# The first S5 block and the first GLA head in written order on VectorE and ScalarE, with their tables loaded early

## The chip, the cores and the metric

One Trainium2 chip, one core. The metric is the time of one execution of the program in device microseconds (us). The median of 3 runs of the kernel before is 879.52 us (878.79 to 879.74). The engines are called PE (TensorE), DVE (VectorE), ACT (ScalarE), POOL (GpSimd) and SP (SyncE); here POOL and SP mostly issue DMAs.

## What is computed

A decoder block on 512 tokens with 16 meta tokens ahead of them, width 1024. One projection `w_in` gives q, k, v, r, a low-rank gate, u and two gates z. Two mixers run beside each other: gated linear attention (GLA, 4 heads) and a grouped complex-diagonal state space model (S5, 64 groups of 16 channels with 64 states). Their outputs are gated and merged, and a squared-ReLU MLP follows.

```
proj = rmsnorm(h) @ w_in
q, k, v, r, a_low, u, z_gla, z_ssm = split(proj)
# GLA, per head and chunk of 64:
b = cumsum(log_a);  q_in = q*exp(b - b_ref);  k_in = k*exp(b_ref - b)
o = tril(q_in @ k_in.T) @ v + (q*exp(b)) @ state
state = exp(b_last)*state + (k*exp(b_last - b)).T @ v
# S5, per group:
x_t = Lbar x_{t-1} + Bbar u_t;   y_t = Re(C x_t) + D u_t
# merge and MLP:
mixed = sigmoid(z_gla)*(norm(o)*silu(r) @ w_o) + sigmoid(z_ssm)*glu(gelu(y))
h = h + rmsnorm(mixed @ w_out);   h = h + rmsnorm(relu(rmsnorm(h) @ w_ff1)**2 @ w_ff2)
```

## The kernel before

All dense products are in fp32 by three passes: each weight tile of 128 columns is loaded raw by SP (`wraw`, three buffers, `raw_w`, L166), split into a high part on ACT (`whi`, L160) and a low part on DVE (`wlo`, L175), and PE multiplies hi by hi, hi by lo and lo by hi of the normalised input `xh`, `xl` (`feat_tile`, `mm3`, L61). One such product, its split and what follows it is a slot: `slot()` takes the next of the list `dense`; `early_slot()` also works off a list of small jobs, each with an estimate of its cost on DVE.

The program has an early phase and a main phase. In the early phase the u, z and low-rank columns are multiplied, while jobs compute the S5 parameters: powers of lambda (written to DRAM as `lamd` by `powers_out`), the input matrix B (`b_bar`, to `bard`), and the decay sums of the heads (`bd`). The order of PE is pinned throughout to the order in which the code is written. The orders of DVE and ACT are pinned in the early phase only: there `V` and `S` are wrappers that keep each instruction in written order. The early phase ends with the two slots that carry `blocks[0].tables()`; then `V, S = nc.vector, nc.scalar`, and a scheduler orders the rows of DVE and ACT from there on. On the chip each engine works through its rows in the order in which they stand.

The main phase is a loop over the 8 S5 blocks of 8 groups each. Beside the first four blocks one GLA head each is computed. Per block:

- `loads` (L1095, L1097): B (512 KB) and lambda's powers `lam` (2 x 256 KB) are read from DRAM, spread over the partitions. Block 0 loads on POOL's queue, all others on SP's.
- `tables` (L1105 to L1119): M2 (a copy and five DVE rows) and M1 (four DVE rows, from B and lam). The tables of a block are computed during the block before.
- `turns` (L1124 to L1130, L235 to L238): `d0` and `E` are filled by ACT, eight loads bring `U`, and twelve DVE rows double `E` three times.
- `kernels` (L1142 to L1145): the local kernel `krow`, to DRAM, and back as M3 on POOL.
- `scan` (L1167 to L1177): `v` from M1 and U, copies `vs` of exchanged halves on ACT, the scan row on DVE (L1172), then X in three rows.

Per head (`Head`): `decays` (L964 to L985) loads `b2` and takes three differences, all in one buffer `d1`, and their exponentials on ACT: `e_gk`, `e_k`, `e_q`, `e_fk`, `e_fq`, `e_dec`; `query_decay` adds `e_gq`. The slots value, value, key, query give `vt`, `kT` and the queries; `key` multiplies kT into `e_gk`, `e_k`, `e_fk` (L997 to L999), `query` the queries into `e_q`, `e_fq`, `e_gq` (L1005 to L1007). `turn_values` and `turn_keys` transpose on PE (L66), `scores` reads `e_k`, `e_q`, `e_fk`, `e_fq`, and `states` the turned keys and values (L1038 to L1053).

On PE, block 0 and head 0 run in this order: value slot, kernels, value slot, scan, key slot, turn_values, query slot, turn_keys, a gate slot, scores and states; then the first value slot of block 1.

SP issues its DMAs in one row too: weight tiles in the order of the slots, and between them U, b2, and B and lam.

Of the kernel before, what the change touches and what calls it, by code (L numbers as in the profile page):

```python
# [10 lines left out]
F32R = mybir.dt.float32r  # L11
# [6 lines left out]
P = 128  # L18
# [19 lines left out]
T8 = 8  # L38
# [12 lines left out]
def hybrid_block(ctx: ExitStack, tc: tile.TileContext, io, out: bass.AP):  # L51
# [814 lines left out]
    def b_bar(c):  # L866
# [8 lines left out]
        if c:  # L875
            for i, half_ in enumerate((low_, high_)):
                nc.gpsimd.dma_start(bard[T8 * i : T8 * i + T8].rearrange("h g n -> g h n"), bar[half_].rearrange("g h c n -> g h (c n)"))

    low_rank()
    gate_weights()  # L880
    ready.update({0: f0, 1: f1})
# [29 lines left out]
    early_slot(2.2, 2.2)  # L911
    early_slot(2.2, 100.0)
    assert not jobs
    sga.close()
    st5.close()

    sgb = ExitStack()
    pgb = pool("pgb", stack=sgb)
# [7 lines left out]
    G.memset(scb[0], 0.0)  # L926
    d0 = mk(b5, [P, GB, NST], tag="d0")
    G.memset(d0, 0.0)
    NS = 80
    metas = [mk(pgb, [NS, DV + P], F32R, tag=f"meta{i}") for i in range(2)]  # L930
    for t in metas:
        S.copy(t, d0[:NS].rearrange("p g c -> p (g c)")[:, : DV + P])

    class Head:

# [17 lines left out]
        def turn_values(self):  # L953
            self.vtok = mk(pgb, [P, TT, DV], tag="vtok", bufs=2)
            for j, vt in enumerate(self.vt):
# [3 lines left out]
                    PE.transpose(ps[:, t * P : (t + 1) * P], vt[:, t * P : (t + 1) * P], ident)  # L959
                S.copy(self.vtok[:, :, cc], ps.rearrange("p (t c) -> p t c", t=TT))  # L960

        def decays(self):
            b2 = mk(pgb, [P, NT], tag="b2")
            nc.sync.dma_start(b2, bd[self.h])  # L964
            bm = b2[:, :SEQ].rearrange("p (c t) -> p c t", t=CH)
            bp = b2[:, :SEQ].rearrange("p (c t) -> p c t", t=P)

            def ex(shape, src, tag, scale):
                e = mk(pgb, shape, tag="e_" + tag)
                S.activation(e, src, AF.Exp, scale=scale)  # L970
# [7 lines left out]
            V.tensor_sub(d1.rearrange("p (c t) -> p c t", t=CH), bm, bm[:, :, 32:33].to_broadcast([P, 8, CH]))  # L978
# [3 lines left out]
            V.tensor_sub(dx, bp, bp[:, :, 63:64].to_broadcast([P, TT, P]))  # L982
# [3 lines left out]
            self.b2, self.ex = b2, ex  # L986

        def query_decay(self):
            self.qg = self.ex([P, SEQ], self.b2[:, :SEQ], "gq", -1.0 / TAU)
# [51 lines left out]
        def states(self):  # L1041
            self.st = []
            for t in range(0, TT, 2):
                pst = bank().rearrange("p (t v) -> p t v", t=2)
                for i in range(t, t + 2):
                    k, v = (self.ktok[:, i - 1, :], self.vtok[:, i - 1, :]) if i else (self.kmeta, self.vmeta)
                    PE.matmul(pst[:, i % 2], k, v, start=True, stop=True)
                for i in range(t, t + 2):
                    st = mk(pgb, [P, DV], tag="st", bufs=4)
                    if i == 0:  # L1050
                        V.tensor_copy(st, pst[:, 0])
                    else:
                        V.scalar_tensor_tensor(st, self.st[-1], self.dec[:, i - 1 : i], pst[:, i % 2], op0=ALU.mult, op1=ALU.add)  # L1053
                    self.st.append(st)

        def outputs(self):
# [27 lines left out]
    class Block:  # L1084
# [6 lines left out]
        def loads(self, queue=nc.sync):  # L1091

            self.B = mk(b5, [P, GB, 2, NST_N], tag="B")
            self.lam = mk(b5, [P, 2, GB, NST_N], tag="lam")
            queue.dma_start(self.B.rearrange("p g c n -> p (g c n)"), bard[:, self.gs, :].rearrange("h g n -> h (g n)").unsqueeze(0).to_broadcast([T8, HG, GB * 2 * NST_N]))  # L1095
            for i in range(2):
                queue.dma_start(self.lam[:, i].rearrange("p g n -> p (g n)"), lamd[i, :, self.gs, :].rearrange("l g n -> l (g n)").unsqueeze(1).to_broadcast([T8, HG, GB * NST_N]))  # L1097

        def tables(self):

# [46 lines left out]
        def scan(self):  # L1147

            M3 = self.M3 = mk(b5, [P, GB, P], tag="M3", bufs=1)
            for sp in range(T8):  # L1150
                s = T8 - 1 - sp
                nc.gpsimd.dma_start(M3[sp * HG : (sp + 1) * HG], kpad[self.gs].rearrange("g h l -> h g l")[:, :, 112 - 16 * s : 240 - 16 * s])
            U, E = self.U, self.E
            v, vs = (mk(b5, [P, GB, NST], tag=t, bufs=1) for t in ("v", "vs"))

            def exchanged(src, gg):

                S.copy(vs[:64, gg], src[64:])
                S.copy(vs[64:, gg], src[:64])
# [12 lines left out]
            V.tensor_tensor_scan(flat, d0.rearrange("p g c -> p (g c)"), flat, 0.0, op0=ALU.mult, op1=ALU.add)  # L1172
            X = self.X = mk(b5, [P, GB, NST], tag="X", bufs=1)
            exchanged(v, slice(0, GB))
            V.tensor_mul(X, v, E[:, 0])
            V.tensor_mul(vs, vs, E[:, 1])
            V.tensor_sub(X, X, vs)  # L1177
# [78 lines left out]
    for kind in ("r0", "r1", "r2", "r3", "r4", "r5", "r6", "r7", "z7", *(f"o{m}" for m in range(KT))):  # L1256
# [10 lines left out]
    assert not jobs and next(first, None) is None  # L1267
    V, S = nc.vector, nc.scalar
    for b, blk in enumerate(blocks):
        this = heads[b] if b < HEADS else None  # L1270
        last = heads[b - 1] if 0 < b <= HEADS else None
        blk.turns()
        following = iter(())
        if b + 1 < NBLK:
            following = blocks[b + 1].tables()
        slot()
        blk.kernels()
        if b:
            blocks[b - 1].output()
# [4 lines left out]
        blk.scan()  # L1284
# [7 lines left out]
        if b:  # L1292
            next(following, None)
        if b < NBLK - 1:
            slot()
        if this:
            this.turn_values()
        if b:
            next(following, None)
        slot()  # L1300
        if this:
            this.turn_keys()
        if not b:
            with tc.issue_after(blk.made.ins):
                next(following, None)
                next(following, None)
# [12 lines left out]
        if this:  # L1319
            this.scores()  # L1320
            this.states()
        if b:
            blocks[b - 1].turn_output()
        next(following, None)
    slot()
    blocks[-1].output()
# [364 lines left out]
```

## Time and profile before

| | |
|---|---|
| median of the runs | 879.52 us (878.79 to 879.74) |
| the profiled execution | 879.33 us |
| its span | 877.4 us |
| granted clock of TensorE, mean | 0.996 |
| PE busy in the span | 864.0 us |
| DVE, ACT, POOL busy | 654.1, 442.6, 122.0 us |
| end of the early phase and block 0, head 0 | about 88 to 140 us of the span |

In the profile a row names the engine, the line, the operation and the tiles (out<-in, without their numbers, so that M is M1 or M2, and d is d0 or d1), then the shapes and the count. In timelines the first column is the start in us from the span's start, the second the duration, and square brackets show how long the engine was idle just before and what released it. The matmuls of a slot are one after another and overlap; the step from start to start is what one costs. DMA issues are rows of SP's and POOL's queues (SPq, POOLq).

### The profile page before, as it was taken

Reading aid. Unit: us, or ns where it says so; the run is one execution under the profiler, and the core shown is the slowest. Engines: PE = TensorE matmul, PEld = TensorE weight load, DVE = VectorE, ACT = ScalarE, POOL = GpSimd, SP = SyncE. Lnnn points to the kernel's source line nnn. Section 1 sums busy time; section 2 is a strip of 40 time slices with the busy share of each in tenths; the row PEclk is TensorE's granted clock in tenths of the full one; section 3 lists DMA queues with packets and bytes.
Section 4 is the critical chain, followed back from the end, with each engine's and each line's share of the span. In section 5 each row is a group of like instructions: output and inputs, shape, how many; then the busy total and the mean of one; then the engine's idle time right before and its main releaser. Section 6 shows DMA issues by size and latency. Waiting matters only on the chain.

```text
span 877.4 us, 13275 instructions
## 1 busy us (share of the span) xinstructions
PE 864.0 (98%) x4824; PEld 739.6 (84%) x4824; DVE 654.1 (75%) x1180; ACT 442.6 (50%) x749; POOL 122.0 (14%) x214
## 2 busy tenths in 40 slices
PE   9999989999999999999999999999999999999996
PEld 8998879998988888888888888988888888888885
DVE  6999988969696789966445765576766677788886
ACT  7677365757664555334334544333222236665763
POOL 1122120131304221342000001021112100000001
PEclk9999999999999999999999999999999999999999
DMA  9776885554555757758545761598999966866564
GB/s 316 236 223 181 214 202 150 133 143 139 138 138 146 231 151 199 209 153 290 156 145 175 234 164 69 171 322 289 338 296 313 322 228 238 266 196 199 172 204 141
DMA packets 166905, 180.57 MB, mean 206 GB/s; under 512 B 18056, under 2 KB 126760, under 8 KB 166840
## 3 DMA queue, kind: packets, MB, share of 16 engines
q1 hardware_dynamic: 147240, 117.00, 45.3%
q0 software_dynamic: 17744, 58.52, 19.8%
q10 hardware_dynamic: 1856, 4.20, 1.4%
q8 instruction: 38, 0.62, 0.3%
q14 instruction: 27, 0.22, 0.1%
HBM read 143.74 MB, written 35.95 MB: 205 GB/s over the span
## 4 chain that ended last, share of the span: by engine, by line
PE 93%; DMA 3%; DVE 2%; issue 1%; ACT 0%; SPq 0%; ACTq 0%; POOL 0%; DVEq 0%
PE mm L61 68%; PE sm L61 23%; PE sm L66 2%; DMA wraw<-in_w_in_dram 2%; DMA lam<-lamd 1%; DVE xT L79 0%; DVE wlo L79 0%; DVE c L1612 0%; DVE c L1606 0%; SPq L1097 0%; DVE M L79 0%; DVE v L1172 0%; DVE B L79 0%; DVE wlo L175 0%; DVE B L1117 0%
## 5 line engine op out<-in xcount | busy, mean ns | idle before, releaser
L160 ACT ACTIVATE whi<-wraw 128x1024 fp32r<-128x1024 f32 x87 | 92.2, 1060 | 224.8 <-PE mm L61 202.6
L175 DVE TENSOR_TENSOR wlo<-wraw,whi 128x1024 fp32r<-128x1024 f32 x87 | 106.4, 1223 | 107.8 <-ACT whi L160 105.8
L61 PE MATMUL mm<-xh,whi 128*128 128x512 f32 (+2 forms) x464 | 159.4, 344 | 0.0
L61 PE MATMUL mm<-xh,wlo 128*128 128x512 f32 (+2 forms) x464 | 156.2, 337 | 0.0
L61 PE MATMUL mm<-xl,whi 128*128 128x512 f32 (+2 forms) x464 | 156.1, 336 | 0.0
L61 PE MATMUL mm<-hh,whi 128*128 128x512 f32 (+1 forms) x280 | 104.0, 371 | 0.0
L61 PE MATMUL mm<-hl,whi 128*128 128x512 f32 (+1 forms) x280 | 103.8, 371 | 0.0
L61 PE MATMUL mm<-hh,wlo 128*128 128x512 f32 (+1 forms) x280 | 103.8, 371 | 0.0
L61 PEld LDWEIGHTS mm<-xh,whi 128*128 128x128 f32 x464 | 88.0, 190 | 9.7 <-issue 1.2
L61 PEld LDWEIGHTS mm<-xh,wlo 128*128 128x128 f32 x464 | 87.8, 189 | 9.2
L61 PEld LDWEIGHTS mm<-xl,whi 128*128 128x128 f32 x464 | 87.9, 189 | 8.5
L1549 DVE TENSOR_TENSOR wlo<-wraw,whi 128x1024 fp32r<-128x1024 f32 x56 | 68.4, 1223 | 20.3 <-ACT whi L1545 20.3
L61 PE MATMUL sm<-wlo,fh 128*128 128x512 f32 x192 | 74.8, 390 | 0.0
L61 PE MATMUL sm<-whi,fh 128*128 128x512 f32 x192 | 74.7, 389 | 0.0
L61 PE MATMUL sm<-whi,fl 128*128 128x512 f32 x192 | 74.7, 389 | 0.0
L1545 ACT ACTIVATE whi<-wraw 128x1024 fp32r<-128x1024 f32 x56 | 58.6, 1049 | 16.8 <-PE mm L61 11.7
L61 PEld LDWEIGHTS mm<-hh,wlo 128*128 128x128 f32 x280 | 52.7, 188 | 9.1
L61 PEld LDWEIGHTS mm<-hl,whi 128*128 128x128 f32 x280 | 52.8, 188 | 9.0
L61 PEld LDWEIGHTS mm<-hh,whi 128*128 128x128 f32 x280 | 52.8, 188 | 9.0
L160 ACT ACTIVATE fh<-f 128x512 fp32r<-128x512 f32 x48 | 30.3, 631 | 45.0 <-PE sm L61 29.9
L61 PE MATMUL mm<-gh,whi 128*128 128x512 f32 x128 | 49.8, 389 | 0.0
L61 PE MATMUL mm<-gl,whi 128*128 128x512 f32 x128 | 49.8, 389 | 0.0
(408 smaller groups left out, 1777.3 us busy)
## 6 DMA issues: line engine op xcount, KB each, us to landing
wraw<-in_w_ff_dram SPq DMA_DIRECT2D x56, 512.0 KB, 4.6
wraw<-in_w_in_dram SPq DMA_DIRECT2D x46, 512.0 KB, 4.1
w2raw<-in_w_ff_dram POOLq DMA_DIRECT2D x16, 1024.0 KB, 8.8
t2d<-w2t POOLq DMA_DIRECT2D x16, 1024.0 KB, 5.9
wraw<-t2d SPq DMA_DIRECT2D x32, 512.0 KB, 4.0
wraw<-in_w_glu_dram SPq DMA_DIRECT2D x16, 512.0 KB, 4.3
M<-kpad POOLq DMA_DIRECT2D x64, 64.0 KB, 2.6
wraw<-in_w_o_gla_dram SPq DMA_DIRECT2D x8, 512.0 KB, 6.2
```

Source lines behind the costliest of these rows:

```text
L61: ins = nc.tensor.matmul(*args, **kw)
L66: ins = nc.tensor.transpose(*args, **kw)
L160: S.activation(dst, src, AF.Copy, scale=scale)
L175: V.tensor_sub(lo, raw, f32(hi))
L1545: halved = S.activation(bh, raw, AF.Copy)
L1549: V.tensor_sub(bl, raw, f32(bh))
```

## The change

- Written order goes on. The lines `V, S = nc.vector, nc.scalar` move behind a new function `first_block()`, which holds block 0, head 0 and block 1's tables. So the rows of DVE and ACT in it stand in the order in which it is written. PE's rows are the same as before.
- B and lam of block 0 get places of their own (`B0`, `lam0`, in the early pool `pga`) and are loaded by two jobs on POOL's queue behind `powers_out` and `b_bar`. Where block 0's loads were, on POOL, block 1's are now. The early pool is closed, and the pool of the heads opened, after the first tables.
- `decays` loses the load of b2 to `decay_load`; `scan` is split in two by a `yield` behind the scan row.
- In the loop, which begins with block 1, `turns` and `decays` are issued behind `heads[0].held`, the last state row of head 0; the old condition `blk.made` of the decays is gone.

```diff
+    B0 = mk(pga, [P, GB, 2, NST_N], tag="B0")
+    lam0 = mk(pga, [P, 2, GB, NST_N], tag="lam0")
...
     jobs.append((0.0, powers_out))
     jobs.extend((2.0, lambda c=c: b_bar(c)) for c in range(2))
+    jobs.append((0.0, lambda: lam_load(0, lam0, nc.gpsimd)))
+    jobs.append((0.0, lambda: b_load(0, B0, nc.gpsimd)))
...
-    blocks[0].loads(nc.gpsimd)
+    blocks[0].B, blocks[0].lam = B0, lam0
+    blocks[1].loads(nc.gpsimd)
     first = blocks[0].tables()
...
+    def first_block():
+
+        blk, this, following = blocks[0], heads[0], blocks[1].tables()
+        this.decay_load()
+        blk.turns()
+        slot()
+        this.decays()
+        blk.kernels()
+        slot()
+        next(following)
+        next(following)
+        steps = blk.scan()
+        next(steps)
+        this.query_decay()
+        slot()
+        next(steps, None)
+        this.turn_values()
+        next(following)
+        next(following)
+        slot()
+        this.turn_keys()
+        slot()
+        this.scores()
+        this.states()
+
+    first_block()
     V, S = nc.vector, nc.scalar
     for b, blk in enumerate(blocks):
+        if not b:
+            continue
...
-        blk.turns()
+        with tc.issue_after(heads[0].held.ins):
+            blk.turns()
...
-            with tc.issue_after(blk.made.ins), tc.issue_after(this.taken.ins):
+            this.decay_load()
+            with tc.issue_after(this.taken.ins), tc.issue_after(heads[0].held.ins):
                 this.decays()
```

How the rows of the engines move, at three places. First ACT, from the end of the early phase on. Before (the two casts fill the meta tiles of the heads, `d` is d0, and `E` the input of block 0's turns):

```order
L1126 COPY E_1403<-E_16_112 128x16x9
L79 ACTIVATE ut_1292<-mm_1267 128x512
L79 CAST meta_203_1311<-d_202_1309 80x384
L79 CAST meta_204_1312<-d_202_1309 80x384
L79 ACTIVATE whi_1322<-wraw_1320 128x1024
L79 COPY M_210_1325<-CA_107 128x8x16
L1124 COPY d_202_1309<-prm_110 128x8x64
L1105 COPY M_279_1753<-CA_107 128x8x16
L79 ACTIVATE ut_1362<-mm_1337 128x512
L79 ACTIVATE whi_1367<-wraw_1365 128x1024
L79 ACTIVATE ut_1399<-mm_1374 128x512
```

ACT at the same place in the change:

```order
L79 COPY M_210_1322<-CA_107 128x8x16
L79 ACTIVATE ut_1359<-mm_1334 128x512
L79 ACTIVATE whi_1364<-wraw_1362 128x1024
L79 ACTIVATE ut_1396<-mm_1371 128x512
L79 CAST meta_221_1403<-d_204_1310 80x384
L79 CAST meta_222_1404<-d_204_1310 80x384
L79 COPY d_204_1310<-prm_110 128x8x64
L79 COPY E_1410<-E_16_112 128x16x9
L79 ACTIVATE whi_1441<-wraw_1439 128x1024
```

The casts, d0 and E now stand behind the split of the tile of the second value slot (whi_1364, before whi_1367) and the last copy of the gates (ut_1396, before ut_1399).

Second DVE at the end of the scan, before (`M_278`, `B_1621` are block 1's M1 and B; the first wlo is the split for the gate slot, the last that for block 1's first value slot):

```order
L175 TENSOR_TENSOR wlo_1632<-wraw_1628,whi_1630 128x1024
L1167 TENSOR_TENSOR v_1594<-sm_1604,E_1403 128x260
L1115 TENSOR_TENSOR M_278_1752<-B_1621,lam_1622 128x1024
L1169 TENSOR_TENSOR vs_1595<-vs_1595,E_1403 128x520
L1117 TENSOR_TENSOR B_1621<-B_1621,lam_1622 128x1024
L1170 TENSOR_TENSOR v_1594<-v_1594,vs_1595 128x520
L1118 TENSOR_TENSOR M_278_1752<-M_278_1752,B_1621 128x8x64
L1172 SCALAR_TENSOR_TENSOR v_1594<-d_202_1309,v_1594 128x520
L1119 TENSOR_TENSOR M_278_1752<-M_278_1752,B_1621 128x8x64
L1175 TENSOR_TENSOR X_1615<-v_1594,E_1403 128x520
L175 TENSOR_TENSOR wlo_1707<-wraw_1703,whi_1705 128x1024
L1176 TENSOR_TENSOR vs_1595<-vs_1595,E_1403 128x520
```

DVE at the same place in the change, up to the row of the keys:

```order
L79 TENSOR_TENSOR M_256_1591<-M_256_1591,mta_1597 128x4x128
L79 TENSOR_TENSOR v_1609<-sm_1611,E_1410 128x260
L79 TENSOR_TENSOR v_1609<-sm_1619,E_1410 128x260
L79 TENSOR_TENSOR vs_1610<-vs_1610,E_1410 128x520
L79 TENSOR_TENSOR v_1609<-v_1609,vs_1610 128x520
L79 SCALAR_TENSOR_TENSOR v_1609<-d_204_1310,v_1609 128x520
L79 TENSOR_TENSOR wlo_1636<-wraw_1632,whi_1634 128x1024
L79 TENSOR_TENSOR e_gk_1501<-kT_1638,e_gk_1501 128x528
```

The M1 and B rows of block 1 and X have left the stretch; the last row of block 1's M2 (M_256) stands just ahead of it.

Third DVE from e_gk on, before (`E_1830` belongs to block 1's turns):

```order
L997 TENSOR_TENSOR e_gk_1510<-kT_1634,e_gk_1510 128x528
L1177 TENSOR_TENSOR X_1615<-X_1615,vs_1595 128x520
L998 TENSOR_TENSOR e_k_1514<-kT_1634,e_k_1514 128x512
L999 TENSOR_TENSOR e_fk_1520<-kT_1634,e_fk_1520 128x256
L235 TENSOR_TENSOR mta_1841<-E_1830 128x128
L236 TENSOR_TENSOR epb_1842<-E_1830 128x128
L237 TENSOR_TENSOR E_1830<-mta_1841,epb_1842 128x8x8
L238 TENSOR_TENSOR E_1830<-mta_1841,epb_1842 128x8x8
L235 TENSOR_TENSOR mta_1847<-E_1830 128x256
L1005 SCALAR_TENSOR_TENSOR e_q_1516<-mm_1709,e_q_1516 128x512
L1006 SCALAR_TENSOR_TENSOR e_fq_1522<-mm_1709,e_fq_1522 128x256
```

DVE from e_gk on in the change (`M_255`, `B_1312` are block 1's M1 and B, wlo_1721 is the split for its first value slot):

```order
L79 TENSOR_TENSOR e_gk_1501<-kT_1638,e_gk_1501 128x528
L79 TENSOR_TENSOR e_k_1505<-kT_1638,e_k_1505 128x512
L79 TENSOR_TENSOR e_fk_1511<-kT_1638,e_fk_1511 128x256
L79 TENSOR_TENSOR X_1694<-v_1609,E_1410 128x520
L79 TENSOR_TENSOR vs_1610<-vs_1610,E_1410 128x520
L79 TENSOR_TENSOR X_1694<-X_1694,vs_1610 128x520
L79 TENSOR_TENSOR M_255_1590<-B_1312,lam_1313 128x1024
L79 TENSOR_TENSOR B_1312<-B_1312,lam_1313 128x1024
L79 TENSOR_TENSOR M_255_1590<-M_255_1590,B_1312 128x8x64 x2
L79 TENSOR_TENSOR wlo_1721<-wraw_1717,whi_1719 128x1024
L79 SCALAR_TENSOR_TENSOR e_q_1507<-mm_1723,e_q_1507 128x512
L79 SCALAR_TENSOR_TENSOR e_fq_1513<-mm_1723,e_fq_1513 128x256
```

X, the M1 and B rows of block 1 and the split of a tile now stand between the products of the keys and those of the queries; block 1's turns stand behind the states of head 0.

More of the change, by code (lines that the diff above doesn't have):

```diff
@@ L877, in b_bar, with b_load, lam_load @@
                 nc.gpsimd.dma_start(bard[T8 * i : T8 * i + T8].rearrange("h g n -> g h n"), bar[half_].rearrange("g h c n -> g h (c n)"))
+    B0 = mk(pga, [P, GB, 2, NST_N], tag="B0")
+    lam0 = mk(pga, [P, 2, GB, NST_N], tag="lam0")
+    def b_load(blk, dst, queue):
+        gs = slice(blk * GB, (blk + 1) * GB)
+        queue.dma_start(dst.rearrange("p g c n -> p (g c n)"), bard[:, gs, :].rearrange("h g n -> h (g n)").unsqueeze(0).to_broadcast([T8, HG, GB * 2 * NST_N]))
+    def lam_load(blk, dst, queue):
+        gs = slice(blk * GB, (blk + 1) * GB)
+        for i in range(2):
+            queue.dma_start(dst[:, i].rearrange("p g n -> p (g n)"), lamd[i, :, gs, :].rearrange("l g n -> l (g n)").unsqueeze(1).to_broadcast([T8, HG, GB * NST_N]))
     low_rank()
@@ L928, in hybrid_block @@
     G.memset(d0, 0.0)
[L929 to L932, printed above, removed]
     class Head:
@@ L1052, in states @@
                     else:
-                        V.scalar_tensor_tensor(st, self.st[-1], self.dec[:, i - 1 : i], pst[:, i % 2], op0=ALU.mult, op1=ALU.add)
+                        self.held = V.scalar_tensor_tensor(st, self.st[-1], self.dec[:, i - 1 : i], pst[:, i % 2], op0=ALU.mult, op1=ALU.add)
                     self.st.append(st)
@@ L1094, in loads @@
             self.lam = mk(b5, [P, 2, GB, NST_N], tag="lam")
-            queue.dma_start(self.B.rearrange("p g c n -> p (g c n)"), bard[:, self.gs, :].rearrange("h g n -> h (g n)").unsqueeze(0).to_broadcast([T8, HG, GB * 2 * NST_N]))
-            for i in range(2):
-                queue.dma_start(self.lam[:, i].rearrange("p g n -> p (g n)"), lamd[i, :, self.gs, :].rearrange("l g n -> l (g n)").unsqueeze(1).to_broadcast([T8, HG, GB * NST_N]))
+            b_load(self.blk, self.B, queue)
+            lam_load(self.blk, self.lam, queue)
         def tables(self):
@@ L1267, in hybrid_block @@
     assert not jobs and next(first, None) is None
+    sga.close()
+    sgb = ExitStack()
+    pgb = pool("pgb", stack=sgb)
+    NS = 80
+    metas = [mk(pgb, [NS, DV + P], F32R, tag=f"meta{i}") for i in range(2)]
+    for t in metas:
+        S.copy(t, d0[:NS].rearrange("p g c -> p (g c)")[:, : DV + P])
+    def first_block():
[22 more added lines that the diff above has]
+    first_block()
     V, S = nc.vector, nc.scalar
     for b, blk in enumerate(blocks):
+        if not b:
+            continue
         this = heads[b] if b < HEADS else None
         last = heads[b - 1] if 0 < b <= HEADS else None
-        blk.turns()
+        with tc.issue_after(heads[0].held.ins):
+            blk.turns()
         following = iter(())
@@ L1291, in hybrid_block @@
                 this.query_decay()
-        if b:
-            next(following, None)
+        next(following, None)
         if b < NBLK - 1:
@@ L1297, in hybrid_block @@
             this.turn_values()
-        if b:
-            next(following, None)
+        next(following, None)
         slot()
@@ L1302, in hybrid_block @@
             this.turn_keys()
[L1303 to L1306, printed above, removed]
         if last:
```

20 lines of the change are left out of this document (9 added, 11 removed).

## The prediction, made before the changed kernel was run

> **What bounds the kernel now.** The views were read in this order: the page, the chain that ended last, PE's waits, then PE's timeline at the one wait that matters, and last the timelines of DVE, ACT and SP ahead of it. The page gives the bound: PE is busy 98% of the span, and the chain is PE's by 93%.
>
> ```profile
> span 877.4 us, 13275 instructions
> PE 864.0 (98%) x4824; PEld 739.6 (84%) x4824; DVE 654.1 (75%) x1180; ACT 442.6 (50%) x749; POOL 122.0 (14%) x214
> ...
> PE 93%; DMA 3%; DVE 2%; issue 1%; ACT 0%; SPq 0%; ACTq 0%; POOL 0%; DVEq 0%
> ```
>
> So only PE's waits are to be had. The view of PE's waits has two rows (us in total, times, longest):
>
> ```profile
> PE sm L66 <- DVE e_gk L997: 4.0, 1, 4.0
> PE sm L61 <- DVE xss L513: 1.3, 1, 1.3
> ```
>
> The second lies at 1.3 us, which the change doesn't reach. The first is PE's turn of the first head's keys (turn_keys), which waits for e_gk. PE's timeline there (start, duration, engine, line, tiles, count, in brackets the idle time before):
>
> ```profile
> 119.09 1.13 PE L66 MATMUL sm<-ident,vt 128*128 128x128 f32 x8
> 119.97 0.47 PE L61 MATMUL mm<-xh,whi 128*128 128x512 f32 x1
> ...
> 129.90 1.02 PE L66 MATMUL sm<-ident,e_gk 128*16 128x128 f32 x4 [4.00 <-DVE e_gk L997]
> ```
>
> PE stood ready at 129.90 - 4.00 = 125.90. The windows around it (length, PE, PEld, DVE, ACT, POOL, granted clock, DMA share, GB/s) show that the wait also cost clock: 0.54 in the 3.5 us behind it, 1.00 later.
>
> ```profile
> 129.90:133.40 3.50, 3.50 (x11) 2.98 (x12) 3.43 (x10) 2.24 (x5) 0.00 (x0) 0.54 0.76 222
> 133.40:138.00 4.60, 4.60 (x33) 3.62 (x34) 4.51 (x10) 0.72 (x1) 0.00 (x0) 1.00 0.55 181
> ```
>
> The chain of waits prices it. The same gate product takes 6.55 us here and 5.49 in the next block (the first row is a weight tile that is spoken of below):
>
> ```profile
> 107.06 11.22 DMA wraw<-in_w_in_dram
> ...
> 130.92 6.55 PE mm L61 x24
> 137.47 2.69 PE sm L61 x31
> ...
> 173.60 5.49 PE mm L61 x24
> ```
>
> Without wait, scores() would begin at 125.90 + 0.44 (four turns; the eight at 119.09 took 0.88 to the next start) + 5.49 = 131.83. It began at 137.47. **5.64 us are to be had**, and no more.
>
> Why was e_gk late? DVE and SP each take their rows in order. In the rows of DVE, M1 of block 0 waits 1.91 us for lam, and later a split waits 3.38 us for ACT, which waits for a weight tile:
>
> ```profile
> 98.67 1.23 DVE L79 TENSOR_TENSOR M<-B,lam 128x1024 f32<-128x1024 f32 x1 [1.91 <-DMA lam<-lamd]
> 99.81 0.28 DVE L235 TENSOR_TENSOR mta<-E 128x128 f32<-128x128 f32 x1
> ...
> 105.81 1.22 DVE L1108 TENSOR_TENSOR M<-CA,Lr 128x1024 f32<-128x1024 f32 x1
> ...
> 108.60 0.42 DVE L238 TENSOR_TENSOR E<-mta,epb 128x256 f32<-128x256 f32 x1
> ...
> 119.48 1.22 DVE L175 TENSOR_TENSOR wlo<-wraw,whi 128x1024 fp32r<-128x1024 f32 x1 [3.38 <-ACT whi L160]
> ...
> 125.05 1.23 DVE L1172 TENSOR_TENSOR_SCAN v<-d,v 128x520 f32<-128x520 f32 x1
> ...
> 126.79 0.69 DVE L1175 TENSOR_TENSOR X<-v,E 128x520 f32<-128x520 f32 x1
> 127.40 1.22 DVE L175 TENSOR_TENSOR wlo<-wraw,whi 128x1024 fp32r<-128x1024 f32 x1
> 128.53 0.69 DVE L1176 TENSOR_TENSOR vs<-vs,E 128x520 f32<-128x520 f32 x1
> 129.14 0.70 DVE L997 TENSOR_TENSOR e_gk<-kT,e_gk 128x528 f32<-128x528 f32 x1
> ```
>
> **The change, part by part.** *What goes.* M1 of block 0 no longer waits, since B0 and lam0 are loaded while the dense slots run: 1.91 us of DVE's wait. SP no longer holds three B and lam loads ahead of the weight tile of the gate, which took 11.22 us and set the 3.38 us wait. So both causes of the delay go; the question is what is late next.
>
> *What does not go.* The loads that stood on POOL at 87.81 and 89.69 are replaced by block 1's, of the same bytes at the same places. The weight tile issued at 88.25 shares the engines with them and with eight U loads:
>
> ```profile
> 88.25 0.37 SPq L166 DMA_DIRECT2D wraw<-in_w_in_dram  x1
> ...
> 89.30 12.83 SPq L1130 DMA_DIRECT2D U<-ud  x8
> ```
>
> ACT's row shows when it is there, and two more rows that the sum needs (E and d are the inputs of the turns):
>
> ```profile
> 84.64 0.32 ACT L1126 COPY E<-E 128x144 f32<-128x144 f32 x1 [0.37 <-DVE E L79]
> ...
> 88.71 0.91 ACT L79 CAST meta<-d 80x384 fp32r<-80x384 f32 x2
> ...
> 90.68 0.62 ACT L1124 COPY d<-prm 128x512 f32<-128x512 f32 x1
> ...
> 101.03 1.06 ACT L79 ACTIVATE whi<-wraw 128x1024 fp32r<-128x1024 f32 x1 [6.79 <-DMA wraw<-in_w_in_dram]
> 102.00 0.58 ACT L79 ACTIVATE ut<-mm 128x512 f32<-128x512 f32 x1
> ```
>
> The page's row of these loads has their median, issue to landing:
>
> ```profile
> wraw<-in_w_in_dram SPq DMA_DIRECT2D x46, 512.0 KB, 4.1
> ```
>
> I keep 101.0 for the landing, 12.8 us behind the issue. Its bounds are that median, 4.1 us (92.4), and the end of the U issues that share the engines (89.30 + 12.83 = 102.1).
>
> *What is added: the first stall.* ACT now follows the written order, so E is copied behind that split, not at 84.64. From 102.00: ut 0.47 (to the next start), casts 0.91, d 0.52, E 0.32, so 104.2. The twelve DVE rows of the turns follow in one piece. In the trace before the twelve lie between 99.81 and 109.0, from four of 128 or 64 wide (0.28 and less) to four of 512 or 256 wide (0.68, 0.42), and add up to 4.6 us; next starts come some 0.03 to 0.07 ahead of ends, so in one piece they take 4.2, to 108.4. The key's split takes 1.13 (127.40 to 128.53) to 109.6. Then the decays: three subtractions on one buffer d1, each of which waits for the exps of the one before. These rows of ACT give the exps (e_q is as wide as e_k) and a copy of the scan:
>
> ```profile
> 109.37 0.65 ACT L970 ACTIVATE e_gk<-d 128x528 f32<-128x528 f32 x1
> ...
> 113.57 0.63 ACT L970 ACTIVATE e_k<-d 128x512 f32<-128x512 f32 x1 [2.35 <-DVE d L978]
> ...
> 115.79 0.42 ACT L970 ACTIVATE e_fk<-d 128x256 f32<-128x256 f32 x1 [0.81 <-DVE d L982]
> ...
> 121.59 0.37 ACT L1159 COPY vs<-sm 64x260 f32<-64x260 f32 x1
> ```
>
> Back to back: 0.9 + 0.65 + 0.7 + 1.15 + 0.7 + 1.0 (e_fk, e_fq, dec, krow) + 0.5 (two krow rows) gives 115.2; with the query's hi and lo splits, some of it alongside, 116.9. The five M2 rows of block 1 stand here now: 1.13 + 4 x 0.7 = 3.9, so 120.8. Scan: two products of 0.35 (half as wide as vs), 1.2 for ACT's copies of vs, of which two of 0.37 lie wholly behind the second product, vs 0.65, v 0.65, scan 1.23: 125.2. The gate's split 1.13, and e_gk 0.70: **127.0**. PE wants it at 125.90: a stall of **1.1 us**. The table load of exp lies beside the turns and costs nothing while they last.
>
> Nothing else of DVE lies in that stretch: as the rows in the section on the change show, the four M1 and B rows of block 1 have left it (some 3.6 us that the path would otherwise carry) and stand behind e_gk.
>
> *What is added: the second stall.* The query rows e_q and e_fq, which scores() reads, now stand behind X, block 1's M1 and B and a split (the second pair of rows in the section on the change). With 0.65 for a 512-wide row and 1.2 for a 1024-wide one: from e_gk's start 0.7 + 0.65 + 0.35 + 3 x 0.68 + 2 x 1.2 + 2 x 0.65 + 1.13 + 0.68 = 9.2; by the shorter start-to-start steps it is 8.7, and I take 9.0. So e_q is done at 126.3 + 9.0 = 135.3. PE, released at 127.0, gets there at 127.0 + 0.44 + 5.49 = 132.9: **a stall of 2.3 us**. For e_fq (0.4) and the two meta rows behind it I add 0.5, part of them beside the matmuls. This stall doesn't depend on when e_gk comes, as long as e_gk is what PE waits for.
>
> *The sum.* Lost after: 1.1 + 2.3 + 0.5 = 3.9; before: 5.64. Gain 1.74 at the profiled execution's 879.33 us (span 877.4 and 1.9 around it): 877.6. The median of the runs, 879.52, lies 0.2 above, so 877.8; the sum has no waits between rows of different engines, for which I add 0.1: **877.9**.
>
> The 0.54 clock stood behind a 4.0 us wait. [...]
>
> **What moves in block 1.** Its turns and decays now wait for the last state (held). In the rows before they begin behind e_fk. Some 4.5 us of turns and 0.9 of d rows move behind 140. The window of block 1 has room on DVE, and its own e_gk comes early:
>
> ```profile
> 140.00:172.00 32.00, 32.00 (x258) 29.98 (x257) 27.56 (x58) 21.63 (x47) 5.34 (x10) 1.00 0.47 126
> ```
>
> ```profile
> 168.85 0.70 DVE L997 TENSOR_TENSOR e_gk<-kT,e_gk 128x528 f32<-128x528 f32 x1
> ```
>
> ```profile
> 172.07 1.53 PE sm L66 x14
> ```
>
> 4.4 us are idle, and e_gk of block 1 ends at 169.55, 2.9 us before PE, whose turns begin at 172.07 with two of the values, reads it at about 172.45. 5.4 against 7.3: I cost it at nothing; with none of the idle time usable it costs 5.4 - 2.9 = 2.5.
>
> **Rivals.** *The tile at 88.25 lands earlier* (99 or before). What speaks for it is that 8.7 of the 12.8 us are above the median; against it, the same bytes are in flight. Then e_gk is in time and only e_q is late: its chain starts 2 us earlier, 133.3 + 0.5 against 131.83, so 2.0 lost, 3.6 gained, 875.9. With 3 us (ACT then waits for PE's 98.87 slot no longer) 874.9.
>
> *Slower: the tile lands later*, because U and the decay rows go into the queues beside it in another order. PE itself reads the split at 105.44, the start of the second value slot:
>
> ```profile
> 105.44 0.39 PE L61 MATMUL mm<-xh,whi 128*128 128x256 f32 x1
> ```
>
> The lo split ends 2.3 us after landing, so from 103.1 on PE waits there too. Each us later costs one; by 1.7 us the gain is gone. At 3.5 us: 1.4 there, then 3.2 and 2.8: 7.4, so 1.8 slower than before, 881.3, and with the half clock behind a 3.2 us wait 882.4.
>
> *Block 1 stalls* for the moved turns: 877.9 + 2.5 = 880.4. *No change*: the weight tiles wait for their buffers, so e_gk comes as late as it did, 879.5.
>
> **How the numbers follow.** Forecast 0.45 (own range 876.8 to 879.2), early tile 0.22, late tile 0.15, block 1 stall 0.10, no change 0.08. 0.2% is 1.76 us, about what a measurement of this kernel can tell from no change: 877.76 to 881.28. Faster: 0.22 and half of the forecast, 0.43. Slower: most of the late tile and a little of block 1, 0.14. Same: 0.43. Range 875.0 to 882.0.
>
> **What would show it.** In PE's waits: e_gk with about 1.1 us, and a new row of about 2.3 us at the scores for e_q; clock 1.00 behind both. In ACT's timeline E behind the split of the tile that lands at 101; in DVE's no wait for lam. A single PE wait above 3.4 us, a wait for wlo at 105, or one in block 1 would make the prediction wrong; so would a weight tile at 88 that lands before 99.

## The result: 880.16 us, a little slower

The changed kernel's median is 880.16 us (878.99 to 882.36, 20 runs) against 879.50 (877.21 to 881.48, 20 runs) for the kernel before. The ratio is 1.0011, 95% interval 1.0003 to 1.0019: slower by 0.1%, where 877.9 was forecast. The range held the time; the sign did not.

The page of the changed kernel, the lines that answer to those of before:

```profile
span 879.0 us, 13271 instructions
PE 864.2 (98%) x4824; PEld 739.3 (84%) x4824; DVE 655.1 (75%) x1180; ACT 441.4 (50%) x749; POOL 123.8 (14%) x217
```

PE's waits, total us, times, longest. Where there were two rows there are seven:

```profile
PE sm L61 <- DVE e_q L79: 2.3, 1, 2.3
PE sm L66 <- DVE e_gk L79: 1.6, 1, 1.6
PE sm L61 <- DVE xss L513: 1.3, 1, 1.3
PE sm L61 <- DVE xrs L79: 0.6, 1, 0.6
PE sm L61 <- ACT whi L79: 0.5, 1, 0.5
PE mm L61 <- DVE wlo L79: 0.5, 1, 0.5
PE sm L61 <- DVE meta L79: 0.4, 1, 0.4
```

The wait of 4.0 for e_gk became one of 1.6 for e_gk and one of 2.3 for e_q, both where the prediction put them. The rest it did not have. Where PE stood at three places in the program is read best from its timeline, first of the kernel before, then of the changed one. The rows are block 0's kernels, and block 1's first matmul:

```profile
104.85 0.66 PE L61 MATMUL sm<-M,BA 128*32 128x128 f32 x16
```

```profile
139.81 0.47 PE L61 MATMUL mm<-xh,whi 128*128 128x256 f32 x1
```

```profile
89.55 0.50 PE L61 MATMUL mm<-xh,wlo 128*128 128x512 f32 x1 [0.47 <-DVE wlo L79]
...
106.09 0.66 PE L61 MATMUL sm<-M,BA 128*32 128x128 f32 x16
...
128.69 0.62 PE L66 MATMUL sm<-ident,e_gk 128*16 128x128 f32 x4 [1.61 <-DVE e_gk L79]
...
137.13 0.30 PE L61 MATMUL sm<-e_q,e_k 128*64 128x64 f32 x2 [2.34 <-DVE e_q L79]
...
138.79 0.54 PE L61 MATMUL sm<-meta 80*128 80x256 f32 x1 [0.38 <-DVE meta L79]
139.13 2.76 PE L61 MATMUL sm<-vtok,ktok 128*128 128x256 f32 x6
141.33 0.78 PE L61 MATMUL mm<-xh,whi 128*128 128x256 f32 x1
```

PE comes to block 0 already 1.24 us late; at the scores it is 0.27 ahead of the kernel before (137.13 against 137.40), so 1.5 were won in between; and at block 1 it is 1.52 late (141.33 against 139.81). So some 1.8 were lost within the scores and states, of which the wait for meta explains 0.38. The windows say what the rest is (the seventh number is the granted clock):

```profile
134.80:137.10 2.30, 0.00 (x0) 0.00 (x0) 2.30 (x4) 2.27 (x3) 0.00 (x0) 1.00 0.34 124
...
139.00:141.00 2.00, 2.00 (x6) 1.64 (x7) 1.96 (x3) 0.00 (x0) 0.00 (x0) 0.50 0.71 186
141.00:144.00 3.00, 3.00 (x21) 2.82 (x20) 2.81 (x5) 0.00 (x0) 0.00 (x0) 0.80 1.10 230
```

TensorE's clock was halved again (0.50 in 139.00 to 141.00), as it was behind the wait of 4.0 us in the kernel before (0.54 in the 3.5 us behind it), now behind a wait of 2.34 us.

Of the early loss of 1.24, 0.55 is PE's wait for xrs at 27 us, and 0.47 its wait at 89.55. What made the second: VectorE's row of the decay sums waits for a buffer whose store to DRAM took 6.13 us (the median of these stores in the kernel before is 2.4), and the split wlo that PE needs at 89.55 stands behind it. From the changed kernel's chain of waits, then from its DVE timeline, then the kernel before at the same row:

```profile
79.63 6.13 DMA bd<-b
```

```profile
85.79 1.45 DVE L79 TENSOR_TENSOR_SCAN b<-mn,ga 128x128 f32<-128x128 f32 x5 [0.66 <-DMA bd<-b]
```

```profile
84.53 1.45 DVE L79 TENSOR_TENSOR_SCAN b<-mn,ga 128x128 f32<-128x128 f32 x5
```

2.9 us ahead of that store, at 76.70, POOL issued the load of B0:

```profile
76.70 0.61 POOL L884 DMA_DIRECT2D B<-bard  x1 [0.65 <-DMA bard<-bar]
```

### The profile page after: what moved, and what is told of

Same layout as the page of the kernel before. It is cut to its first block, busy times and chain, and to the rows that moved or that the text cites. A ratio compares the mean times of both kernels' runs of the same rounds, so it can differ in the third digit from the quotient of the medians.

```text
span 879.0 us, 13271 instructions
## 1 busy us (share of the span) xinstructions
PE 864.2 (98%) x4824; PEld 739.3 (84%) x4824; DVE 655.1 (75%) x1180; ACT 441.4 (50%) x749; POOL 123.8 (14%) x217
## 4 chain that ended last, share of the span: by engine, by line
PE 88%; DVE 5%; DMA 3%; ACT 2%; issue 1%; SPq 1%; POOL 0%; ACTq 0%; DVEq 0%; POOLq 0%
PE mm L61 64%; PE sm L61 22%; PE sm L66 2%; DMA xt<-in_x_dram 1%; DVE wlo L79 1%; DMA bard<-bar 1%; DMA bd<-b 1%; DMA wraw<-in_w_in_dram 1%; DVE M L79 0%; DVE mta L79 0%; SPq L488 0%; DVE xT L79 0%; DVE d L79 0%; DVE c L1655 0%; ACT whi L79 0%
## 5 line engine op out<-in xcount | busy, mean ns | idle before, releaser
L160 ACT ACTIVATE whi<-wraw 128x1024 fp32r<-128x1024 f32 x82 | 86.9, 1060 | 214.0 <-PE mm L61 189.2
L175 DVE TENSOR_TENSOR wlo<-wraw,whi 128x1024 fp32r<-128x1024 f32 x82 | 100.3, 1223 | 101.6 <-ACT whi L160 101.4
L1592 DVE TENSOR_TENSOR wlo<-wraw,whi 128x1024 fp32r<-128x1024 f32 x56 | 68.4, 1223 | 19.3 <-ACT whi L1588 19.1
L1588 ACT ACTIVATE whi<-wraw 128x1024 fp32r<-128x1024 f32 x56 | 58.6, 1048 | 16.0 <-PE mm L61 11.7
```

The lines of the kernel that those rows point to most:

```text
L160: S.activation(dst, src, AF.Copy, scale=scale)
L175: V.tensor_sub(lo, raw, f32(hi))
L1588: halved = S.activation(bh, raw, AF.Copy)
L1592: V.tensor_sub(bl, raw, f32(bh))
```

## The experiments

All were timed in five rounds beside the kernel before; ratios are to it, with their 95% intervals.

**The tail alone.** The last two steps of block 1's tables behind the states.

```diff
         this.turn_values()
-        next(following)
-        next(following)
         slot()
...
         this.states()
+        next(following)
+        next(following)
```

> The changed kernel with the last two steps of block 1's tables (M1 and B, four VectorE rows, 3.7 us) written behind head 0's states instead of ahead of the query slot. Theory A (the loss is the scores' wait for e_q, 2.34 us, the wait for meta behind it, 0.38, and the half clock that follows them, about 1.5): all three go, the wait for e_gk of 1.6 stays, and the time is about 4.2 us below the changed kernel, 876 us. Theory B (the loss lies in the early phase, where the early loads hold up the decay sums, and in block 1, where turns and decays now wait for the last state): at most 1 us, 879 to 880, and a new wait of PE in block 1 since the M1 rows come later.

877.12 us, 0.9970 (0.9959 to 0.9981), about 3 us below the changed kernel. Both waits at the scores and the half clock are gone (1.00 in every window from 130 to 144); e_gk's 1.47 stays. But there is a new wait in block 1, the only one of PE between 130 and 180:

```profile
170.36 1.50 PE L66 MATMUL sm<-ident,on 128*128 128x128 f32 x8 [0.99 <-ACT on L1083]
```

So theory A holds for the scores, though 3.0 us were won and not 4.2, and B for about 1 us: block 1 had no room for the moved rows.

**The decay sums.** Three buffers for b instead of two.

```diff
-        b2 = mk(pga, [P, NT], tag="b2", bufs=2)
+        b2 = mk(pga, [P, NT], tag="b2", bufs=3)
```

> The changed kernel with three buffers instead of two for the decay sums on their way to DRAM. In the changed kernel's profile VectorE waits 0.66 us for a buffer whose store took 6.1 us beside the early loads, and PE then waits 0.47 us for a low split. Theory A: PE's wait at 89.6 goes, 0.5 to 0.7 us less, about 879.5; nothing else moves. Theory B (the early loads are the whole cause): back to the kernel before, 877 to 879.5, with the wait for e_gk gone as well.

879.41 us, 0.9996 (0.9988 to 1.0005). PE's wait at 89 is gone, and block 0's kernels stand at 104.84 as before the change. The waits for e_gk (1.49) and e_q (2.37) stay, and here the half clock lasted longer:

```profile
134.00:136.00 2.00, 0.23 (x2) 0.27 (x2) 2.00 (x4) 1.97 (x3) 0.00 (x0) 0.85 0.41 144
136.00:138.00 2.00, 2.00 (x25) 1.88 (x25) 1.94 (x4) 0.22 (x1) 0.57 (x1) 0.50 0.32 79
138.00:140.00 2.00, 2.00 (x6) 1.64 (x6) 1.96 (x4) 0.00 (x0) 0.00 (x0) 0.50 0.91 219
140.00:142.00 2.00, 2.00 (x9) 1.82 (x9) 1.85 (x4) 0.00 (x0) 0.00 (x0) 0.50 0.95 214
```

It fell while PE was still waiting (0.85 in 134 to 136) and lasted 6.8 us, twice the changed kernel's 3.4. The median is 0.75 below the changed kernel's 880.16 (1.3 by the two ratios), about what theory A gave the store alone, and not clear of the kernel before. B, with e_gk's wait gone, falls.

**The gap filled.** Ten matmuls of 512 columns ahead of head 0's scores.

```diff
             pv = ps.rearrange("p (t c) -> p t c", t=TT)
+            if not self.h:
+                for i in range(10):
+                    PE.matmul(ps, xh[:, 0, :P], xh[:, 0, :SEQ], start=True, stop=True)
             for t in range(TT):
```

> The changed kernel with ten extra matmuls of 512 columns (some 2.3 us of PE, their result is overwritten or never read) ahead of head 0's scores, where PE waits 2.34 us for e_q. Theory A (the clock was halved because PE stood idle too long in a short time): the scores begin no later than before, the clock stays at 1.00 behind them, and the states and the next value slot take 1.4 to 1.6 us less: about 878.6. Rival (the clock fell for another reason, or these matmuls have another limit): clock 0.5 as before, 880.2 or more.

879.93 us, 1.0004 (0.9995 to 1.0012): 0.2 to 0.8 below the changed kernel (880.16, and 880.73 when it was run again), less than expected and not clear of noise by its time. The trace is clear. Scores begin at 137.16 (the changed kernel: 137.13), and from there:

```profile
138.91 0.36 PE L61 MATMUL sm<-meta 80*128 80x256 f32 x1 [0.38 <-DVE meta L79]
139.10 1.46 PE L61 MATMUL sm<-vtok,ktok 128*128 128x256 f32 x6
140.21 0.47 PE L61 MATMUL mm<-xh,whi 128*128 128x256 f32 x1
```

```profile
138.00:140.00 2.00, 1.62 (x19) 1.40 (x18) 1.94 (x5) 0.00 (x0) 0.57 (x1) 1.00 0.37 63
140.00:142.00 2.00, 2.00 (x17) 1.95 (x16) 1.92 (x5) 0.00 (x0) 0.00 (x0) 1.00 0.99 263
```

The clock stays at 1.00, and the six state rows take 1.46 us instead of 2.76; the next slot begins 1.12 earlier. And in ten of this kernel's eleven runs the mean granted clock is 0.997 to 0.999 (once 0.995), where the changed kernel's twenty have 0.993 to 0.997. So with PE busy in the gap the clock was not halved, as theory A has it. That the median gained less is taken up at the changed kernel's second profile.

**The loads alone.** B0, lam0 early, block 1's loads on POOL, but the main loop from block 0 on in the scheduler's order. The steps of block 1's tables go back to their places of before, too (the diff leaves them out, and the function itself).

```diff
...
-    first_block()
     V, S = nc.vector, nc.scalar
     for b, blk in enumerate(blocks):
-        if not b:
-            continue
...
+            with tc.issue_after(blk.made.ins), tc.issue_after(this.taken.ins):
+                this.decay_load()
+                this.decays()
...
-            blocks[b + 1].loads()
+        if 0 < b and b + 1 < NBLK:
+            blocks[b + 1].loads()
```

> The early loads alone: B0 and lam0 in places of their own, block 1's loads on POOL where block 0's were, the pools opened as in the change, but VectorE and ScalarE ordered by the scheduler from the main loop on, as in the kernel before. Theory A (both causes of e_gk's delay were loads, and the written order is what adds new waits): VectorE's waits of 1.91 and 3.38 us go, e_gk comes about 4 us earlier, PE's wait for it is below 0.5 us: 874.5 to 876. Theory B (the early loads hold up the early phase, and the written order is needed to use them): 879 or more, with e_gk still awaited by over 2 us.

876.31 us, 0.9962 (0.9950 to 0.9974). One half of the change is worth 3.3 us; the whole is worth nothing. PE waits 1.43 for e_gk, more than expected, and not at all at the scores. It waits 1.69 for the split behind the decay sums:

```profile
91.05 0.50 PE L61 MATMUL mm<-xh,wlo 128*128 128x512 f32 x1 [1.69 <-DVE wlo L79]
...
130.01 0.62 PE L66 MATMUL sm<-ident,e_gk 128*16 128x128 f32 x4 [1.43 <-DVE e_gk L1008]
```

**The loads alone, with three buffers** for the sums.

```diff
-        b2 = mk(pga, [P, NT], tag="b2", bufs=2)
+        b2 = mk(pga, [P, NT], tag="b2", bufs=3)
```

> The early loads alone, as in the run before without written order, and three buffers for the decay sums. There PE waited 1.69 us for a low split that stood behind a store of the sums. Theory A (that store is what the early loads cost): the wait goes, PE reaches block 0 earlier by it, the wait for e_gk becomes 1.4 to 3, since the weight tiles are only partly tied to it: 874.3 to 875.8. Theory B (the early loads cost nothing, the 1.69 was chance): 876.3 as without.

874.63 us, 0.9940 (0.9927 to 0.9953), 1.7 below the run without. PE's wait at 91 is gone; the one for e_gk is 1.35. Theory A.

**The order alone.** No B0 and lam0 and no jobs for them; the loads of blocks 0 and 1 on POOL and SP as before the change.

```diff
-    blocks[0].B, blocks[0].lam = B0, lam0
-    blocks[1].loads(nc.gpsimd)
+    blocks[0].loads(nc.gpsimd)
...
         blk.kernels()
         slot()
+        blocks[1].loads()
         next(following)
```

> The written order alone: first_block() as in the change, but block 0's B and lam loaded on POOL where they were before, and block 1's on SP behind the second value slot. Theory A (the two halves of the change act apart: the loads remove e_gk's waits, the order adds its own): M1 of block 0 waits about 2 us for lam again, and with e_q behind block 1's tables the time is above the kernel before, 880.5 to 883. Theory B (the early loads are what hurts): 878 to 879, below the changed kernel.

880.21 us, 1.0007 (0.9998 to 1.0016): the changed kernel's time within the noise, 0.3 below theory A's range and not clear of the kernel before. No wait at 89, since the early loads are absent; in their place VectorE's M1 waits 1.96 us for lam, e_gk 2.01, e_q 2.37, meta 0.38:

```profile
98.48 1.23 DVE L79 TENSOR_TENSOR M<-B,lam 128x1024 f32<-128x1024 f32 x1 [1.96 <-DMA lam<-lamd]
```

```profile
127.66 0.62 PE L66 MATMUL sm<-ident,e_gk 128*16 128x128 f32 x4 [2.01 <-DVE e_gk L79]
136.10 0.30 PE L61 MATMUL sm<-e_q,e_k 128*64 128x64 f32 x2 [2.37 <-DVE e_q L79]
```

The clock was halved here as well, for 3.4 us: by its mean of 0.62 in this window from 137.7 on, and the value slot's matmuls of 256 columns are back at a step of 0.12 us at 141.2:

```profile
137.00:140.00 3.00, 2.62 (x17) 2.15 (x13) 2.91 (x6) 0.00 (x0) 0.43 (x1) 0.62 0.65 137
```

Taking the wait for lam away, 1.96 us, shortens the wait for e_gk by 0.4 only (2.01 to 1.61), and even that is PE coming later: VectorE's row of e_gk starts at 126.90 here and at 127.93 in the changed kernel. In both runs the turns wait for E (0.41 and 0.94 us), which ScalarE copies behind the split of the tile issued at 88 or 89, so with the written order M1's wait is beside the path. The early loads then cost 0.5 at 89. As far as these traces go, that is why the two halves of the change don't add up.

**The tail and the sums** together.

```diff
-        b2 = mk(pga, [P, NT], tag="b2", bufs=2)
+        b2 = mk(pga, [P, NT], tag="b2", bufs=3)
...
         this.states()
+        next(following)
+        next(following)
```

> The changed kernel with M1 and B of block 1 behind the states and three buffers for the decay sums. With M1 moved alone it was 877.1, with waits of 1.5 for e_gk, 1.0 in block 1 and 0.4 for a low split at 89. Theory A: the last goes, 876.3 to 877.0. Theory B (e_gk is tied to the weight tiles and not to PE): the wait for e_gk grows by what was saved, 877.1.

876.07 us, 0.9959 (0.9946 to 0.9972). The wait at 89 is gone, e_gk's is 1.10, that in block 1 is 0.99 as before. Theory A, 0.2 below its range.

**The turns ahead.** Block 0's E and its first two doublings before the split that waits for the tile, the third behind it. To the tail and the sums together (the method `first_turns`, which takes these rows out of `turns`, is left out):

```diff
+    jobs.insert(3, (2.1, blocks[0].first_turns))
+    jobs.append((2.1, lambda: erot(blocks[0].E, 32, 32, b5)))
-    early_slot(2.2, 2.2)
+    early_slot(2.2, 4.0)
     early_slot(2.2, 100.0)
```

> The kernel before this one (M1 and B of block 1 behind the states, three buffers), and block 0's turns ahead: E is copied and doubled twice on VectorE ahead of the split that waits for the weight tile, once behind it, where twelve rows stood behind it. Theory A (the wait for e_gk that is left comes from the written order, which puts the turns behind that tile): e_gk comes 2 to 3 us earlier, its wait goes, 874.5 to 875.5. Rival (it comes from the buffer d1, through which the decays pass one by one, and from the tiles): the wait stays above 1 us, 876 to 877.

876.00 us, 0.9957 (0.9944 to 0.9970): no gain, and theory A falls. VectorE did the turns early and then waited as long for the key's tile:

```profile
108.16 1.23 DVE L79 TENSOR_TENSOR wlo<-wraw,whi 128x1024 fp32r<-128x1024 f32 x1 [2.62 <-ACT whi L79]
```

In the run before this split stood at nearly the same time, behind the turns:

```profile
108.09 1.23 DVE L79 TENSOR_TENSOR wlo<-wraw,whi 128x1024 fp32r<-128x1024 f32 x1 [0.20 <-ACT whi L79]
```

So in that kernel the turns and the tile, which SP issues behind the U loads, were ready within 0.2 us of each other, and taking one away leaves the other. In the changed kernel itself the turns are the later of the two. From its second profile (told below), ScalarE's split of the tile, then VectorE's last rows of the turns and the split behind them:

```profile
107.31 1.06 ACT L79 ACTIVATE whi<-wraw 128x1024 fp32r<-128x1024 f32 x1 [2.10 <-DMA wraw<-in_w_in_dram]
```

```profile
108.82 0.76 DVE L79 TENSOR_TENSOR E<-mta,epb 128x256 f32<-128x256 f32 x2
109.50 1.22 DVE L79 TENSOR_TENSOR wlo<-wraw,whi 128x1024 fp32r<-128x1024 f32 x1
```

The tile's high part is there at 108.37, and VectorE comes to its split 1.1 us later without a wait (in the first profile 1.6 later, 109.75 against 108.11). The turns ahead were not tried on the changed kernel.

**M1 behind the keys**, without written order. To the loads with three buffers:

```diff
-            V.tensor_mul(self.kg, kT, self.kg)
+            self.keyed = V.tensor_mul(self.kg, kT, self.kg)
...
-        next(following, None)
+        with ExitStack() if b else tc.issue_after(this.keyed.ins):
+            next(following, None)
```

(the second at both places where block 1's M1 is made).

> The early loads and the three buffers without written order (874.6, PE waits 1.35 us for e_gk), and block 1's M1 and B issued behind the keys' row e_gk; the scheduler then puts X ahead of e_gk and M1, B behind it. Theory A (what is left of the wait is VectorE's work ahead of e_gk): the wait shrinks by 1.2 or more, the scores still don't wait, 873.3 to 874.0. Rival (e_gk is tied to ScalarE's copies of kT and vs or to the tile of the gate): 874.6 with the wait as it was; or M1, late now, makes PE wait in block 1: above 874.6.

873.43 us, 0.9928 (0.9914 to 0.9941): the fastest of all, 7.0 us below the median beside it (6.3 by the ratio), and theory A. PE doesn't wait for e_gk any more; what is left in the program's middle is 0.35 us for meta.

```profile
PE sm L61 <- DVE xss L513: 1.3, 1, 1.3
PE sm L61 <- DVE meta L1032: 0.4, 1, 0.4
PE sm L61 <- DVE wlo L79: 0.2, 1, 0.2
```

**Block 1's loads on SP**, as before the change, to the loads with three buffers.

```diff
-    blocks[1].loads(nc.gpsimd)
...
-        if 0 < b and b + 1 < NBLK:
+        if b + 1 < NBLK:
             blocks[b + 1].loads()
```

> The early loads of block 0 and the three buffers without written order, but block 1's B and lam on SP's queue ahead of the gate's tile, where they stood before the change, so that POOL moves nothing of theirs at 88. Theory A (of the two delays of e_gk it was the wait for lam and its traffic that counted): the tile issued at 88 lands some 2 us earlier, and since B0 is a place of its own SP no longer waits for M1: 873.5 to 875, no worse than with the loads on POOL. Theory B (the three loads on SP ahead of the gate's tile were the cause): the gate's tile lands at 115 or later, VectorE waits over 2 us for its split, the wait for e_gk is above 2.5: 876 to 878.

874.08 us, 0.9937 (0.9924 to 0.9951). Theory A: without block 1's traffic on POOL the tile issued at 88 lands sooner, and SP passes the eight U loads behind it in 5.5 us. In the run just told the eight took SP 12.03 us, and ScalarE split the tile at 100.21; here it does at about 94.5 (its next row starts at 99.40 after 3.89 us of idle, and a split takes 1.06), 5.8 earlier, where 2 us were expected. First SP's row in the run just told, then here:

```profile
88.41 12.03 SPq L1140 DMA_DIRECT2D U<-ud  x8
101.36 0.39 SPq L166 DMA_DIRECT2D wraw<-in_w_in_dram  x1
```

```profile
90.95 5.52 SPq L1140 DMA_DIRECT2D U<-ud  x8
96.57 0.46 SPq L166 DMA_DIRECT2D wraw<-in_w_in_dram  x1
```

The key's tile is issued 4.8 us earlier, and PE waits 0.20 for e_gk. So in this run the three loads on SP, with places that need not wait for M1, did no harm.

**The changed kernel again.**

> The changed kernel as it is, to hold it against the others on one chip. Theory A (the scores' wait and the half clock behind it are in every execution, the waits of 0.5 at 6.7 and 27 us are not): waits for e_gk of 1.3 to 1.8, e_q 2.3 to 2.4, half clock behind the scores; 879.5 to 880.5. Rival (the profiled execution was unlike the others): no half clock, under 879.

880.73 us, 1.0011 (1.0001 to 1.0021). The waits repeat: 0.55 at 89, e_gk 1.52, e_q 2.36, meta 0.38. The clock does not:

```profile
134.00:137.00 3.00, 0.64 (x5) 0.25 (x3) 3.00 (x6) 2.58 (x3) 0.00 (x0) 1.00 0.27 89
137.00:140.00 3.00, 2.62 (x32) 2.29 (x31) 2.94 (x6) 0.35 (x1) 0.57 (x1) 1.00 0.27 63
140.00:143.00 3.00, 3.00 (x26) 2.97 (x26) 2.81 (x6) 0.00 (x0) 0.00 (x0) 1.00 0.96 284
```

The time is 0.2 above theory A's range, and neither theory had that: behind the same wait (2.34 and 2.36 us) the clock was 0.50 in one execution and 1.00 in the other. And with PE that much earlier, block 1 makes it wait:

```profile
173.16 1.50 PE L66 MATMUL sm<-ident,on 128*128 128x128 f32 x8 [0.35 <-ACT on L1083]
```

From block 1's scan (154.52) to its scores (180.05) PE took 25.53 us here; with the half clock in front it was 24.57 (156.37 to 180.94), and 24.59 in the kernel before (154.43 to 179.02). So 0.9 of what the clock takes in one execution, block 1 takes in the other. That could be why the filled gap gained little, but its own profile doesn't show it: from block 1's scan (154.83) to its scores (179.54) PE took 24.71 there, and that execution, 879.37, is 1.4 below the changed kernel's profiled one, 880.76. Why its median gained less stays open.

**Without `held`.** To the tail and the sums together:

```diff
-        with tc.issue_after(heads[0].held.ins):
-            blk.turns()
+        blk.turns()
...
-            with tc.issue_after(this.taken.ins), tc.issue_after(heads[0].held.ins):
+            with tc.issue_after(this.taken.ins):
```

> The changed kernel with M1 and B of block 1 behind the states and three buffers (876.1, PE waits 1.0 us in block 1 for on, which stands behind VectorE's rows), and without the condition that block 1's turns and decays are issued behind the last state. Theory A (that condition crowds VectorE in block 1): the wait for on goes, 0.9 to 1.5 less, 874.6 to 875.2. Rival (the written order itself leaves those rows no earlier place, whatever the condition): the wait stays at 0.7 or more, 875.8 to 876.4.

876.57 us, 0.9972 (0.9962 to 0.9981). The wait for on is 0.99 as it was: the rival, 0.2 above its range. So the condition is not what crowds block 1. That VectorE's rows have no earlier place is what remains, and is not shown by itself.

## Why the prediction was wrong, point by point

- *M1's wait for lam goes*: right, and shown by the run with the order alone, where it is back. But with the written order it gains nothing at e_gk, since the turns wait for E in any case.
- *The first stall, 1.1 at e_gk*: 1.61 and 1.52, by the path that the sum led through. The tile was issued 1.28 later (89.53) and landed as it was taken to (its split stands at 102.24, 1.2 later), and the rows behind it follow the sum, each some 1.3 later as PE is: the turns end at 109.8 (108.4 in the sum), block 1's M2 at 122.1 (120.8). Only the scan took 0.3 more than was given to it, and e_gk ends at 128.6 (127.0), 0.5 more of a stall than forecast. What the prediction didn't see is the second path, 1.1 to 1.6 us behind the first: the key's tile, which lands 5 us later. With three buffers and the tail moved it sets the time as much as the turns do.
- *The second stall, 2.3 at e_q*: 2.34, 2.36, 2.37 and 2.37 in four profiles, by the mechanism that was worked out. The 0.5 for what follows was 0.38 and about 0.2.
- *Full clock behind both waits*: this step failed. Behind a wait of 2.34 to 2.37 us the clock was 0.50 in three of the four profiles that had it, and 1.00 in the fourth. In the changed kernel's it cost some 1.6 us: from the scores to block 1's scan PE took 19.24 us with the half clock, 17.63 in the second profile without. The waits up to 2.01 us in the program's middle kept the clock in every profile: 1.00 in the windows behind them, and a step of 0.23 us from one 512-column matmul to the next where no window was taken. The sum of 877.9 holds nothing for the clock; that was an estimate, and no run shows it, nor the 3.4 us of the prediction's last sentence as a limit. The kernel before had shown only the 0.54 behind 4.0 us, and the changed kernel showed 0.50 behind 2.34.
- *The early loads cost nothing*: this step failed too. The prediction let them run beside the dense slots and named nothing that they delay. They delay the stores of the decay sums, which share POOL's queue and hold two buffers that VectorE waits for in order (one took 6.13 us, where the median before is 2.4, and VectorE waited 0.66). That cost PE 0.47, 0.55, 0.36 and 1.69 us in four of the five profiles with the early loads and two buffers (in the fifth, with the gap filled, PE didn't wait there), none with three buffers, and none without the early loads. The third buffer is worth 1.7 us without written order, and 1.05 with it and the tail moved.
- *Block 1 has room*: failed in size. 4.4 us idle plus 2.9 of slack at e_gk were counted against 5.4, but the rows that become late are those of the reciprocal root ahead of on (in the first profile ScalarE waits 2.63 us for them, in the second PE 0.35 for on), not e_gk. It costs 0.9 where the clock doesn't fall, and nothing where it does, and in the filled gap's profile 0.1.

The miss: the gain of 1.74 lost 0.5 at e_gk, 0.5 to 0.7 at 89, and 0.9 (block 1) to 1.6 (clock), together 1.9 to 2.8, so 0.2 to 1.1 slower than before; measured 0.66. The wait of 0.55 at 27 us, for xrs, is in the changed kernel's first profile and not in its second, and lies ahead of the first row that the change moves (67 us); I don't count it to the change, though neither profile without the early loads has it.

More than the expected gain was there: 3.3 us by the early loads alone, 5 to 7 with a third buffer and, at the upper end, M1 behind the keys. The written order queued the queries behind block 1's tables and spent it.

## What to carry to other kernels

A change that removes a wait should be split before it is judged: here one half was worth 3.3 us and, with one more buffer, 5.3, while the whole measured slower. When rows are pinned in written order, look for each consumer on the bounding engine and count the rows that now stand ahead of its producer; work for the next block belongs behind the last of them. When a transfer is moved earlier, look at every store in its queue whose buffer an engine in written order waits for (here one took 6.13 us), not only at the loads.

## What the runs showed of the hardware

Behind a wait of TensorE of 2.34 to 2.37 us its granted clock was 0.50 in three profiles and 1.00 in a fourth, at the same place with the same wait. The half clock then lasted 3.4 us in two of them (the changed kernel, the order alone) and 6.8 in the third (three buffers), where it set in while TensorE was still waiting (0.85 in 134 to 136). What decides between the two is not shown by these four. With ten matmuls of 512 columns in the gap the clock was 1.00.

The changed kernel's times spread from 878.99 to 882.36, those of the kernel whose middle has no wait above 0.4 from 873.17 to 873.65. The half clock is not all of that spread: with the gap filled and a mean clock of 0.997 to 0.999 in ten of eleven runs, the times still go from 878.58 to 881.52.
